# Attention scores: full-array matmuls with stacked high and low parts, local and context keys in one matmul, two heads' half-array matmuls in a row

## The chip, the core and the metric

The kernel runs on one core of a Trainium2 chip. A core has five engines that each take their instructions in order: TensorE (PE in the profile, its weight loads PEld), VectorE (DVE), ScalarE (ACT), GpSimd (POOL) and SyncE (SP), which here issues most DMAs. The metric is the device time of one execution in microseconds; lower is better.

## What is computed

Two layers over 512 latent tokens (a grid of 8 rows and 64 columns) and 256 context tokens, width 1024. Each layer has a mixer and a gated MLP. The first layer's mixer is a state-space scan beside neighbourhood attention (8 heads of 64 channels), the second's is differential attention (8 heads, each with two sub-heads of 64 channels). All data is float32. The parts that the change touches, cut short:

```
def neighbourhood_attention(q, k, v, k_ctx, v_ctx, rpb):
    # each latent query sees an 8 x 16 window of the grid and all context keys
    s_loc = einsum('bqhd,bjqkhd->bhqjk', q_r, k_r) * dh ** -0.5 + bias
    s_ctx = einsum('bqhd,bkhd->bhqk', q_r, k_ctx) * dh ** -0.5
    p = softmax(concatenate([s_loc, s_ctx], -1))
    return einsum(p_loc, v_r) + einsum(p_ctx, v_ctx)

def dense_attention(q, k, v):            # context queries, context keys
    s = einsum('bqhd,bkhd->bhqk', q, k) * dh ** -0.5
    return einsum('bhqk,bkhd->bqhd', softmax(s), v)

def diff_attend(q, k, v, lam):           # 512 queries, 768 keys
    s = einsum('bqhd,bkhd->bhqk', q, k) * DIFF_SUB_DIM ** -0.5
    p = softmax(s).reshape(b, DIFF_HEADS, 2, lq, nk)
    a = p[:, :, 0] - lam * p[:, :, 1]
    return einsum('bhqk,bkhd->bqhd', a, v)
```

## The kernel before

**Precision by parts.** The matmuls of projections and scores read a rounded 32-bit type (float32r). To keep float32 accuracy an operand is split into a high part (the rounded value) and a low part (the rest), and products are summed as high x high + low x high + high x low. A score has only 64 channels to contract, half of the array's 128 rows. So `split_qk` (neighbourhood) and `d_qk` (differential) stack parts on the rows: for the head on half e, the tile `Q[e]` holds q's high part on that half and its low part on the other, and `Kh[e]` holds k's high part on both halves. One matmul over all 128 rows then gives high x high + low x high. The third product, high q x low k, is a second matmul over the 64 rows of that half alone, with the low parts of both heads in one tile, `Kl`. It is a half-array matmul: 64*128 in the rows of the profile, where the others have 128*128.

**Neighbourhood attention.** The latent tokens are kept column block by column block, so a block of 128 queries needs two consecutive chunks of keys. `na_pair` works on two heads: four blocks of latent queries (local keys, then 256 context keys) and two of context queries (context keys alone), six units in all, each done by `na_unit`. For each head a unit takes a bank of PSUM for `S`, computes the scores segment by segment (L717, L718), adds the bias (L722, `bt`, NEG outside the window), does the softmax (L725 to L728), transposes it in place (L733) and copies it to `Pt` (L742). Both heads' products with V then go into the first head's bank (L750), and `out` copies them to `att` (L768) and stores them. The local segment has 192 keys in the first and last block and 256 in the others. Before, the first head's instructions all stand ahead of the second's.

**Stages.** In the loop over four groups of state-space heads, `ssd_group` of one group, `na_pair` of the group before (pairs 0 to 2) and, as filler, the projections of the next are written in turns. `na_pair` has two PSUM banks there, three for pair 2. The last pair runs after the loop with two banks and three more in turn, beside the output projection. Then come the first gated MLP, the differential attention and the second MLP.

**Differential attention.** `d_qk(h)` projects and rotates q and k of a head one head ahead, and splits them on ScalarE, VectorE and GpSimd. `d_head(h)` takes the 512 queries in four blocks: for each sub-head a tile `dSp` of 768 scores in two matmuls of 512 and 256 keys with `Kh` (L1188) and two with `Kl` (L1191), then the softmax, the difference, transposes and the product with V.

**What sets the order.** A planner orders each engine's instructions at build time by priority (mostly the order in which the code is written), dependences, free buffers and its own estimate of times. `nc.any` lets it choose ScalarE or VectorE for a copy.

Of the kernel before, what the change touches and what calls it, by code (L numbers as in the profile page):

```python
# [21 lines left out]
NX = 512  # L22
# [29 lines left out]
# Engines (ScalarE, VectorE, GpSimd) of a layer norm's affine map, high parts and low parts.  # L52
# [7 lines left out]
class Ring:  # L60
    """Tiles of several pools in turn, as if of one pool."""
# [10 lines left out]
def emit(tc, T):  # L72
# [16 lines left out]
    pmm = Ring(*MM)  # L89

# [343 lines left out]
    # SSD: time steps and decays  # L434
# [234 lines left out]
    # neighbourhood attention  # L669
# [39 lines left out]

    def na_unit(Q, Kh, Kl, V, qo, segs, chunks, bias, out, pool, tp_, nb):  # L710
        n = sum(m for _, m in segs)
        Ss = []
        for e in range(2):
            S = pool[0].tile([128, 512], F32, name="S", tag=pool[1])
            o = 0
            for k0, m in segs:
                nc.tensor.matmul(S[:, o:o + m], Q[e][:, qo:qo + 128], Kh[e][:, k0:k0 + m], start=True, stop=False)  # L717
                nc.tensor.matmul(S[:, o:o + m], Q[e][HALF[e], qo:qo + 128], Kl[HALF[e], k0:k0 + m], start=False, stop=True)  # L718
                o += m
            if bias is not None:  # L720
                m = segs[0][1]
# [3 lines left out]
            nc.vector.tensor_reduce(nm[:, 0:1], S[:, 0:n], axis=AX, op=OP.max, negate=True)  # L725
            nc.scalar.activation(P[:, 0:n], S[:, 0:n], AF.Exp, bias=nm[:, 0:1], accum_out=nm[:, 1:2])
# [3 lines left out]
            o = 0  # L730
            for i, c in enumerate(chunks):
                m = toks[c][1]
                nc.tensor.transpose(PT[0:m, i], P[:, o:o + m], ident)  # L733
                o += m
# [18 lines left out]
    def na_pair(p, q, k, v, pools, tp_=None, nb=2):  # L753
# [17 lines left out]
        for b in range(4):  # L771
            chunks, k0, nl = NA_BLOCKS[b]
            bt = tp_.tile([128, 2, 256], F32, name="bt", bufs=nb // 2)
            nc.sync.dma_start(bt, T["na_bias"][p, b])
            na_unit(*QK, V, 128 * b, [(k0, nl), (512, 256)], chunks + (5, 6), bt,
# [3 lines left out]
        for t in range(2):  # L779
            na_unit(*QK, V, 512 + 128 * t, [(512, 256)], (5, 6), None,  # L780
# [360 lines left out]

    def rot(px, scale, r):
# [10 lines left out]
    def d_qk(h):  # L1153
# [11 lines left out]
        Kh = [dp.tile([128, NT], F32R, name=f"Kh{e}", bufs=2) for e in range(2)]  # L1165
        Kl = dp.tile([128, NT], F32R, name="Kl", bufs=2)
# [6 lines left out]
        Q = [dp.tile([128, NX], F32R, name=f"Q{e}", bufs=2) for e in range(2)]  # L1173
# [3 lines left out]
        return Q, Kh, Kl  # L1177

    def d_head(h, Q, Kh, Kl, V, filler=()):
        filler = iter(filler)  # L1180
        ob = dp.tile([128, 4, 128], F32, name="ob", bufs=3)
        for tt in range(4):
            ts = slice(128 * tt, 128 * tt + 128)
            Ss = [pS.tile([128, 1024], F32, name="dSp", tag="S") for e in range(2)]
            cols = ((0, 512), (512, 256))
# [159 lines left out]
def _na_bias(rpb):  # L1345
    out = np.full((8, 4, 128, 256), NEG, np.float32)
    qi = np.arange(128)
    for b in range(4):
        _, k0, nl = NA_BLOCKS[b]
        qt = 128 * b + qi  # L1350
        kt = k0 + np.arange(nl)
# [6 lines left out]
        g = rpb[:, dr, dc]  # L1358
        out[:, b, :, 256 - nl:] = np.where(ok[None], g, np.float32(NEG))
# [66 lines left out]
```

## Time and profile before

| | us |
|---|---|
| median of 3 runs | 2067.78 |
| fastest and slowest run | 2060.84, 2069.96 |
| the profiled execution: span from the first to the last instruction | 2062.4 |
| in it: PE busy | 1986.9 |
| DVE busy | 1388.2 |
| ACT busy | 897.9 |
| POOL busy | 754.1 |

Of the profiled execution the page gives the span alone. Matmuls are pipelined: the duration of one in the profile is its latency, and several run at once, so what one costs a full queue is the time from its start to the next one's start. In the timeline a row with x2 stands for two matmuls in a row; its first number is the start of the first, and the next row's first number is the start of the one behind. "Idle before" in brackets names what ended an engine's wait.

### The profile page before, as it was taken

How to read it: one execution, taken by the hardware profiler on the slowest of the kernel's cores; microseconds unless marked ns; L12 is line 12 of the kernel's file. 1: busy time of each engine (PE TensorE's matmuls, PEld its weight loads, DVE VectorE, ACT ScalarE, POOL GpSimd, SP SyncE). 2: the span in 40 equal slices, each digit the busy share in tenths (PEclk: the TensorE clock that was granted, in tenths of full speed). 3: DMA queues.
4: the chain of work that ended last, by engine and by line, in shares of the span. 5: the costliest groups of instructions: out<-in, count | busy, mean ns of one | idle time of the engine just before them, and what ended most of it. 6: DMA issues, size and time to landing. Idle time of an engine off the chain costs nothing.

```text
span 2062.4 us, 31227 instructions
## 1 busy us (share of the span) xinstructions
PE 1986.9 (96%) x11992; PEld 1663.9 (81%) x11992; DVE 1388.2 (67%) x2199; ACT 897.9 (44%) x1757; POOL 754.1 (37%) x631
## 2 busy tenths in 40 slices
PE   7999999999998889999999999999999999999998
PEld 5888878888676787788888888888888778888886
DVE  3766565664757987887676677766556876655567
ACT  3545555574532532223222233655655644333332
POOL 2135124243415935444444417521115264222223
PEclk9999999999999999999999999999999999999999
DMA  9335332232523144333343341322112214323231
GB/s 308 120 107 177 98 122 76 72 121 78 202 72 105 54 135 131 116 100 113 102 143 103 102 144 52 121 62 74 57 51 86 87 42 135 113 82 102 82 113 62
DMA packets 109301, 217.60 MB, mean 106 GB/s; under 512 B 27096, under 2 KB 45888, under 8 KB 109152
## 3 DMA queue, kind: packets, MB, share of 16 engines
q1 hardware_dynamic: 98480, 189.44, 28.6%
q0 software_dynamic: 6016, 20.03, 2.9%
q10 hardware_dynamic: 4656, 6.13, 1.0%
q8 instruction: 95, 1.56, 0.3%
q14 instruction: 54, 0.44, 0.1%
HBM read 202.81 MB, written 8.55 MB: 102 GB/s over the span
## 4 chain that ended last, share of the span: by engine, by line
PE 81%; DVE 11%; DMA 3%; issue 2%; POOL 1%; ACT 1%; SPq 0%; DVEq 0%; ACTq 0%; POOLq 0%
PE fpx L292 20%; PE pdn L1015 13%; PE px L292 7%; PE fpc L292 5%; PE pv L308 4%; PE pc L292 3%; PE pz L308 3%; PE po L833 3%; PE pk L292 2%; PE pq L292 2%; PE S L750 2%; PE avp L1212 2%; DVE acc L185 2%; DMA araw<-in_ada_w 2%; PE dSp L1191 2%
## 5 line engine op out<-in xcount | busy, mean ns | idle before, releaser
L139 ACT ACTIVATE whi<-raw 128x1024 fp32r<-128x1024 f32 (+1 forms) x205 | 215.5, 1057 | 447.7 <-PE fpc L292 163.1
L140 DVE TENSOR_TENSOR wlo<-raw,whi 128x1024 fp32r<-128x1024 f32 (+1 forms) x192 | 256.0, 1339 | 164.0 <-ACT whi L139 161.6
L1015 PE MATMUL pdn<-whi,fact 128*128 128x512 f32 x880 | 280.0, 399 | 5.6 <-DVE ev L314 5.6
L316 POOL TENSOR_TENSOR y<-y,ev 128x512 f32<-128x512 f32 x144 | 211.7, 1485 | 197.3 <-DVE ev L314 153.1
L292 PE MATMUL fpx<-ux,whi 128*128 128x512 f32 (+1 forms) x832 | 232.3, 364 | 6.1 <-DVE cv L974 3.3
L292 PE MATMUL fpx<-u,whi 128*128 128x512 f32 (+1 forms) x832 | 227.4, 359 | 2.4 <-DVE cv L974 1.5
L1015 PEld LDWEIGHTS pdn<-whi,fact 128*128 128x128 f32 x880 | 162.5, 188 | 45.1 <-DVE ev L314 7.0
L292 PEld LDWEIGHTS fpx<-ux,whi 128*128 128x128 f32 x832 | 149.4, 192 | 30.7 <-issue 5.3
L1015 PE MATMUL pdn<-wlo,fact 128*128 128x512 f32 x440 | 172.9, 395 | 0.0
L999 POOL TENSOR_TENSOR fact<-cv,fact 128x768 fp32r<-128x768 f32 (+1 forms) x44 | 73.3, 1666 | 272.4 <-ACT fact L998 272.4
L292 PEld LDWEIGHTS fpx<-u,whi 128*128 128x128 f32 x832 | 149.2, 191 | 26.2 <-ACT cv L970 1.6
L292 PE MATMUL fpx<-ux,wlo 128*128 128x512 f32 (+1 forms) x416 | 151.3, 364 | 2.9 <-DVE wlo L140 2.9
L292 PE MATMUL fpx<-u,wlo 128*128 128x512 f32 (+1 forms) x416 | 149.1, 359 | 1.1 <-DVE wlo L140 1.1
L292 PE MATMUL px<-ux,whi 128*128 128x512 f32 x448 | 149.4, 406 | 0.3 <-ACT whi L139 0.2
L185 DVE SCALAR_TENSOR_TENSOR acc<-araw,condp,acc 128x512 f32<-128x512 f32 x140 | 133.1, 976 | 22.8 <-DMA araw<-in_ada_w 22.2
L974 DVE SCALAR_TENSOR_TENSOR cv<-fpx,fcw,cv 128x511 f32<-128x511 f32 x176 | 130.4, 744 | 22.3 <-ACT cv L970 21.0
L138 POOL TENSOR_TENSOR raw<-raw,G 128x1024 f32<-128x1024 f32 x30 | 76.8, 2565 | 173.7 <-DMA raw<-in_w_down 71.8
L292 PE MATMUL fpc<-uc,whi 128*128 128x256 f32 x704 | 130.3, 283 | 2.0 <-DVE uc L362 1.3
L292 PEld LDWEIGHTS fpc<-uc,whi 128*128 128x128 f32 x704 | 112.4, 190 | 6.7 <-DVE uc L362 1.5
L367 POOL TENSOR_TENSOR y<-y,gb 128x256 f32<-128x256 f32 x112 | 103.5, 959 | 28.1 <-PE lntp L346 28.1
L314 DVE SCALAR_TENSOR_TENSOR ev<-pdn,G 128x512 f32<-128x512 f32 x120 | 81.7, 683 | 41.4 <-PE pdn L1015 34.8
L292 PE MATMUL fpc<-uc,wlo 128*128 128x256 f32 x352 | 99.5, 283 | 0.0
(328 smaller groups left out, 4639.2 us busy)
## 6 DMA issues: line engine op xcount, KB each, us to landing
araw<-in_ada_w SPq DMA_DIRECT2D x96, 512.0 KB
raw<-in_w_up SPq DMA_DIRECT2D x88, 512.0 KB
raw<-in_w_down SPq DMA_DIRECT2D x44, 512.0 KB
E<-scr POOLq DMA_DIRECT2D x24, 512.0 KB, 4.7
raw<-in_w_dqk SPq DMA_DIRECT2D x16, 512.0 KB
raw<-in_w_qkv SPq DMA_DIRECT2D x12, 512.0 KB
raw<-in_w_out SPq DMA_DIRECT2D x12, 512.0 KB
raw<-in_w_bc SPq DMA_DIRECT2D x8, 512.0 KB
```

The costliest lines, as they stand in the source:

```text
L138: nc.gpsimd.tensor_tensor(raw, raw, gate, op=OP.mult)
L139: nc.scalar.activation(hi[:, :n], raw[:, :n], AF.Copy)
L140: (eng or nc.vector).tensor_tensor(lo[:, :n], raw[:, :n], hi[:, :n].bitcast(F32), op=OP.subtract)
L185: nc.vector.scalar_tensor_tensor(acc[:, s], raw[:, i], cs, acc[:, s], op0=OP.mult, op1=OP.add)
L292: nc.tensor.matmul(ps, w[wi][:, kc], rhs(kc, ui), start=(i == 0), stop=(i == n - 1))
L308: nc.tensor.matmul(ps, u_dst(u, kc, ui, tt), w[kc // 4][wi][:, kc % 4], start=(i == 0), stop=(i == n - 1))
L314: nc.vector.scalar_tensor_tensor(t, ps, r, Gh, op0=OP.mult, op1=OP.mult)
L316: eng.tensor_tensor(yh, yh, t, op=OP.add)
L367: nc.gpsimd.tensor_tensor(y[:, c:c + 256], y[:, c:c + 256], t[:, c:c + 256], op=op)
L974: nc.vector.scalar_tensor_tensor(dst[:, lo:hi_], src[:, lo + d:hi_ + d], f[:, tap:tap + 1], dst[:, lo:hi_], op0=OP.mult, op1=OP.add)
L999: nc.gpsimd.tensor_tensor(at_[:, 1], val, at_[:, 0].bitcast(F32), op=OP.subtract)
L1015: nc.tensor.matmul(ps, acts[2 * gs[0] + kt][:, ui, 128 * tt:128 * tt + 128], ws[kt][wi][:, 0, o:o + 512], start=(m == 0), stop=(m == 3 * n ...
```

## The change

In `na_unit` both heads' banks are taken at the start. Each head's first matmul (L717) takes local and context keys together, 512 columns, through a two-part access pattern (`keys`), so the local part always has 256 keys; the fourth block's softmax leaves its first 64 columns out (`NA_COLS`), the first block's takes all 512, with NEG in the bias where the window ends. The two half-array matmuls (L718), one for each head, come after both heads' first ones; `behind` is a dependence that only the planner sees, without a semaphore. `na_bias` is filled for 256 keys in every block.

In `d_qk` the roles change: K's tile now has the high part on the head's own half and the low part on the other; `Qh` has q's high part on both halves, and `Ql` q's low part on the head's half and zeros on the other. `d_head` then uses full-array matmuls only, `Qh` and `Ql` against the same `K`. The zero halves are set once, in four tiles that heads use in turn (`Qlow`). Comments are dropped, which moves the line numbers: L717 and L718 become L731 and L733, L1188 and L1191 become L1210.

```
-NA_BLOCKS = [((0, 1), 0, 192), ((1, 2), 64, 256), ((2, 3), 192, 256), ((3, 4), 320, 192)]
+NA_BLOCKS = [((0, 1), 0), ((1, 2), 64), ((2, 3), 192), ((3, 4), 256)]
+NA_COLS = [(0, 512), (0, 512), (0, 512), (64, 448)]
...
+    def behind(later, earlier):
+        tc.add_manual_dep(later.ins, earlier.ins.name,
+                          mybir.DependencyInfo(mybir.DependencyClass.NoSync, mybir.DependencyReason.DATA), reason="issue order")
...
+    def keys(t, rows, k0):
+        v = t[rows, k0:k0 + 256]
+        return bass.AP(tensor=v.tensor, offset=v.offset, ap=[v.ap[0], [NX - k0, 2], [1, 256]])
+
-    def na_unit(Q, Kh, Kl, V, qo, segs, chunks, bias, out, pool, tp_, nb):
-        n = sum(m for _, m in segs)
+    def na_unit(Q, Kh, Kl, V, qo, k0, chunks, bias, out, pool, tp_, nb):
+        ctx = k0 is None
+        c0, n = (512 - 256, 256) if ctx else NA_COLS[qo // 128]
+        kr = (lambda t, rows: t[rows, NX:NT]) if ctx else (lambda t, rows: keys(t, rows, k0))
+        full = slice(0, 128)
+        S2 = [pool[0].tile([128, 512], F32, name="S", tag=pool[1]) for _ in range(2)]
+        so = [S[:, 256:512] if ctx else S for S in S2]
+        for e in range(2):
+            hi = nc.tensor.matmul(so[e], Q[e][:, qo:qo + 128], kr(Kh[e], full), start=True, stop=False)
+        for e in range(2):
+            lo = nc.tensor.matmul(so[e], Q[e][HALF[e], qo:qo + 128], kr(Kl, HALF[e]), start=False, stop=True)
+            behind(lo, hi)
         Ss = []
         for e in range(2):
-            S = pool[0].tile([128, 512], F32, name="S", tag=pool[1])
-            o = 0
-            for k0, m in segs:
-                nc.tensor.matmul(S[:, o:o + m], Q[e][:, qo:qo + 128], Kh[e][:, k0:k0 + m], start=True, stop=False)
-                nc.tensor.matmul(S[:, o:o + m], Q[e][HALF[e], qo:qo + 128], Kl[HALF[e], k0:k0 + m], start=False, stop=True)
-                o += m
+            S = S2[e]
+            sv = S[:, c0:c0 + n]
             if bias is not None:
-                nc.vector.tensor_tensor(S[:, 0:m], S[:, 0:m], bias[:, e, 256 - m:256], op=OP.add)
+                nc.vector.tensor_tensor(S[:, c0:256], S[:, c0:256], bias[:, e, c0:256], op=OP.add)
...
+    Qlow = [[dp.tile([128, NX], F32R, name=f"Ql{i}{e}") for e in range(2)] for i in range(2)]
+    for i in range(2):
+        for e in range(2):
+            nc.gpsimd.memset(Qlow[i][e][HALF[1 - e]].bitcast(F32), 0.0)
...
-            nc.scalar.copy(Kh[e][HALF[e]], rk[HALF[e]])
-            nc.any.tensor_copy(Kh[e][HALF[1 - e]], Kh[e][HALF[e]].bitcast(F32))
-            nc.gpsimd.tensor_tensor(Kl[HALF[e]], rk[HALF[e]], Kh[e][HALF[e]].bitcast(F32), op=OP.subtract)
+            nc.scalar.copy(K[e][HALF[e]], rk[HALF[e]])
+            nc.gpsimd.tensor_tensor(K[e][HALF[1 - e]], rk[HALF[e]], K[e][HALF[e]].bitcast(F32), op=OP.subtract)
...
-            nc.scalar.copy(Q[e][HALF[e]], rq[HALF[e]])
-            nc.vector.tensor_tensor(Q[e][HALF[1 - e]], rq[HALF[e]], Q[e][HALF[e]].bitcast(F32), op=OP.subtract)
+            nc.scalar.copy(Qh[e][HALF[e]], rq[HALF[e]])
+            nc.any.tensor_copy(Qh[e][HALF[1 - e]], Qh[e][HALF[e]].bitcast(F32))
+            nc.vector.tensor_tensor(Ql[e][HALF[e]], rq[HALF[e]], Qh[e][HALF[e]].bitcast(F32), op=OP.subtract)
...
             for e in range(2):
-                for o, m in cols:
-                    nc.tensor.matmul(Ss[e][:, o:o + m], Q[e][:, ts], Kh[e][:, o:o + m], start=True, stop=False)
-            for o, m in cols:
-                for e in range(2):
-                    nc.tensor.matmul(Ss[e][:, o:o + m], Q[e][HALF[e], ts], Kl[HALF[e], o:o + m], start=False, stop=True)
+                for o, m in ((0, 512), (512, 256)):
+                    for i in range(2):
+                        nc.tensor.matmul(Ss[e][:, o:o + m], Q[i][e][:, ts], K[e][:, o:o + m], start=(i == 0), stop=(i == 1))
```

How the planner's order moves, first on the PE at the first unit of the first pair. nQ_2293 and nQ_2294 are the two heads' Q. Before:

```order
L621 MATMUL Sps<-xw,Bt 128x256
L717 MATMUL S<-nKh_2290,nQ_2293 128x192
L718 MATMUL S<-nKl,nQ_2293 128x192
L717 MATMUL S<-nKh_2290,nQ_2293 128x256
L718 MATMUL S<-nKl,nQ_2293 128x256
L717 MATMUL S<-nKh_2291,nQ_2294 128x192
L718 MATMUL S<-nKl,nQ_2294 128x192
L717 MATMUL S<-nKh_2291,nQ_2294 128x256
L718 MATMUL S<-nKl,nQ_2294 128x256
L620 MATMUL Sps<-xw,Bt 128x256
```

and now, on the same engine at the same place:

```order
L629 MATMUL Sps<-xw,Bt 128x256
L731 MATMUL S<-nKh_2290,nQ_2293 128x512
L731 MATMUL S<-nKh_2291,nQ_2294 128x512
L733 MATMUL S<-nKl,nQ_2293 128x512
L733 MATMUL S<-nKl,nQ_2294 128x512
L628 MATMUL Sps<-xw,Bt 128x256
```

Eight matmuls became four, and the change between full and half array is made once where it was made four times. In most later units of the loop the second head's high matmul stands 10 to 17 rows behind the first head's, as the second head's did before, and the two low ones follow it at once.

On the PE at the first block of head 0 of the differential attention, Q_12794 and Q_12795 being the two sub-heads' Q. Before:

```order
L1188 MATMUL dSp<-Kh_12774,Q_12794 128x512
L1188 MATMUL dSp<-Kh_12774,Q_12794 128x256
L1191 MATMUL dSp<-Kl,Q_12794 128x512
L1191 MATMUL dSp<-Kl,Q_12794 128x256
L292 MATMUL pq<-ux,wlo 128x256
```

and now, on the same engine, K_12718 being the first sub-head's K:

```order
L1210 MATMUL dSp<-K_12718,Qh_12735 128x512
L1210 MATMUL dSp<-K_12718,Ql_12562 128x512
L1210 MATMUL dSp<-K_12718,Qh_12735 128x256
L1210 MATMUL dSp<-K_12718,Ql_12562 128x256
L316 MATMUL pv<-wlo,ux 128x256
```

The count is the same, four; the half-array ones are gone, and the two that share a range of columns stand together.

On VectorE, at the preparation of head 0's Q (rq is the rotated q, wlo a weight's low part, dnm the first softmax's maximum). Before:

```order
L1151 TENSOR_TENSOR rq<-rq,qsw 128x512
L140 TENSOR_TENSOR wlo<-raw,whi 128x1024
L1176 TENSOR_TENSOR Q_12794<-rq,Q_12794 64x512
L1176 TENSOR_TENSOR Q_12795<-rq,Q_12795 64x512
L1196 TENSOR_REDUCE dnm<-dSp 128x1
```

and now, on the same engine:

```order
L1173 TENSOR_TENSOR rq<-rq,qsw 128x512
L148 TENSOR_TENSOR wlo<-raw,whi 128x1024
L1198 TENSOR_TENSOR Ql_12562<-rq,Qh_12735 64x512
L1197 CAST Qh_12735<-Qh_12735 64x512
L1198 TENSOR_TENSOR Ql_12563<-rq,Qh_12736 64x512
L1197 CAST Qh_12736<-Qh_12736 64x512
L1215 TENSOR_REDUCE dnm<-dSp 128x1
```

Two copies have come in between the subtractions and the first softmax.

## Rows read from the trace of the kernel before

**Rows 1.** The page: the span, and each engine's busy time and share.

```profile
span 2062.4 us, 31227 instructions
...
PE 1986.9 (96%) x11992; PEld 1663.9 (81%) x11992; DVE 1388.2 (67%) x2199; ACT 897.9 (44%) x1757; POOL 754.1 (37%) x631
```

**Rows 2.** Stretches: length, busy PE, PEld, DVE, ACT, POOL, then clock, DMA share, GB/s.

```profile
210.00:540.00 330.00, 325.67 (x2064) 270.87 (x2062) 205.30 (x453) 192.42 (x463) 112.90 (x144) 0.99 0.31 100
540.00:630.00 90.00, 89.18 (x437) 67.38 (x437) 48.26 (x97) 36.04 (x91) 21.36 (x17) 0.96 0.37 122
690.00:1345.00 655.00, 631.07 (x3667) 542.21 (x3668) 500.47 (x683) 219.00 (x354) 297.52 (x211) 0.98 0.36 113
1345.00:1640.00 295.00, 293.54 (x1815) 244.28 (x1814) 193.11 (x270) 173.65 (x380) 74.39 (x41) 1.00 0.20 62
```

**Rows 3.** Timeline, PE, differential attention: start, length (us), line, out<-in, array, shape, count.

```profile
1381.31 0.40 PE L292 MATMUL dpc<-uc,whi 128*128 128x256 f32 x2
1381.55 0.51 PE L1188 MATMUL dSp<-Kh,Q 128*128 128x512 f32 x2
1381.99 0.61 PE L1191 MATMUL dSp<-Kl,Q 64*128 64x512 f32 x2
1382.53 0.39 PE L292 MATMUL dpc<-uc,wlo 128*128 128x256 f32 x1
1382.76 0.40 PE L292 MATMUL dpc<-uc,whi 128*128 128x256 f32 x2
```

**Rows 4.** Timeline of the same stretch, the PE's weight loads.

```profile
1381.43 0.31 PEld L1188 LDWEIGHTS dSp<-Kh,Q 128*128 128x128 f32 x2
1381.99 0.29 PEld L1191 LDWEIGHTS dSp<-Kl,Q 64*128 64x128 f32 x2 [0.25 <-issue]
```

**Rows 5.** Timeline, PE, a projection in the differential attention.

```profile
1386.31 0.62 PE L292 MATMUL pq<-ux,whi 128*128 128x512 f32 x2
1386.76 0.39 PE L292 MATMUL pq<-ux,wlo 128*128 128x512 f32 x1
```

**Rows 6.** Timeline, PE, the second unit of the first pair, and the third's start.

```profile
234.61 0.39 PE L717 MATMUL S<-nKh,nQ 128*128 128x256 f32 x1
...
235.87 0.38 PE L292 MATMUL pc<-uc,wlo 128*128 128x256 f32 x1
236.09 0.40 PE L292 MATMUL pc<-uc,whi 128*128 128x256 f32 x2
...
238.31 0.36 PE L717 MATMUL S<-nKh,nQ 128*128 128x256 f32 x1
...
253.00 0.39 PE L717 MATMUL S<-nKh,nQ 128*128 128x256 f32 x1
```

**Rows 7.** Timeline, PE, one head of a unit of context queries.

```profile
310.94 0.28 PE L717 MATMUL S<-nKh,nQ 128*128 128x256 f32 x1
311.15 0.38 PE L718 MATMUL S<-nKl,nQ 64*128 64x256 f32 x1
311.46 0.39 PE L292 MATMUL pc<-uc,whi 128*128 128x256 f32 x1
311.69 0.28 PE L292 MATMUL pc<-uc,wlo 128*128 128x256 f32 x1
```

**Rows 8.** Timeline, PE, where both sub-heads' half-array matmuls stand in a row.

```profile
1588.49 0.62 PE L1191 MATMUL dSp<-Kl,Q 64*128 64x512 f32 x4
1589.04 0.73 PE L1261 MATMUL dpo<-whi,dact 128*128 128x512 f32 x2
```

**Rows 9.** Line L1191: count, least/median/greatest ns, first and last start, forms.

```profile
L1191 PE MATMUL dSp<-Kl,Q x128: 271/438/501, 1350.3 to 1635.0; 64*128 64x512 f32 x64, 64*128 64x256 f32 x64
```

**Rows 10.** Lines on ACT and DVE, as rows 9; then POOL's timeline.

```profile
L768 ACT COPY att<-S x24: 238/266/278, 234.8 to 625.5; 128x128 f32<-128x128 f32 x24
L1175 ACT CAST Q<-rq x16: 616/618/622, 1347.8 to 1597.9; 64x512 fp32r<-64x512 f32 x16
L725 DVE TENSOR_REDUCE nm<-S x48: 412/616/692, 218.3 to 613.1; 128x1 f32<-128x448 f32 x16, 128x1 f32<-128x512 f32 x16, 128x1 f32<-128x256 f32 x16
1333.54 1.30 POOL L1150 TENSOR_TENSOR qsw<-qsw,rope 128x512 f32<-128x512 f32 x1 [22.57 <-DVE wlo L140]
```

More of the change, by code (lines that the diff above doesn't have):

```diff
@@ L708, in split_qk @@
         return Q, Kh, Kl
[L710 to L711 removed]
+    def keys(t, rows, k0):
[13 more added lines that the diff above has]
+            behind(lo, hi)
         Ss = []
         for e in range(2):
[L714 to L719 removed]
+            S = S2[e]
+            sv = S[:, c0:c0 + n]
             if bias is not None:
[L721 to L722 removed]
+                nc.vector.tensor_tensor(S[:, c0:256], S[:, c0:256], bias[:, e, c0:256], op=OP.add)
             P = tp_.tile([128, 512], F32, name="P", bufs=nb)
             nm = tp_.tile([128, 2], F32, name="nm", bufs=2 * nb)
[L725 to L726 removed]
+            nc.vector.tensor_reduce(nm[:, 0:1], sv, axis=AX, op=OP.max, negate=True)
+            nc.scalar.activation(P[:, 0:n], sv, AF.Exp, bias=nm[:, 0:1], accum_out=nm[:, 1:2])
             nc.vector.reciprocal(nm[:, 1:2], nm[:, 1:2])
@@ L729, in na_unit @@
             PT = S.rearrange("p (c q) -> p c q", q=128)
-            o = 0
             for i, c in enumerate(chunks):
-                m = toks[c][1]
+                t0, m = toks[c]
+                o = (t0 - (256 if t0 >= NX else k0)) - c0
                 nc.tensor.transpose(PT[0:m, i], P[:, o:o + m], ident)
-                o += m
             Pt = tp_.tile([128, 4, 128], F32, name="Pt", bufs=nb)
@@ L771, in na_pair @@
         for b in range(4):
-            chunks, k0, nl = NA_BLOCKS[b]
+            chunks, k0 = NA_BLOCKS[b]
             bt = tp_.tile([128, 2, 256], F32, name="bt", bufs=nb // 2)
             nc.sync.dma_start(bt, T["na_bias"][p, b])
-            na_unit(*QK, V, 128 * b, [(k0, nl), (512, 256)], chunks + (5, 6), bt,
+            na_unit(*QK, V, 128 * b, k0, chunks + (5, 6), bt,
                     lambda av: out(128 * b, av),
@@ L779, in na_pair @@
         for t in range(2):
-            na_unit(*QK, V, 512 + 128 * t, [(512, 256)], (5, 6), None,
+            na_unit(*QK, V, 512 + 128 * t, None, (5, 6), None,
                     lambda av: out(512 + 128 * t, av), pools[t % len(pools)], tp_, nb)
@@ L1164, in d_qk, with d_head @@
         ct_x(pq, w, u, 2 if h < 2 else 1)
-        Kh = [dp.tile([128, NT], F32R, name=f"Kh{e}", bufs=2) for e in range(2)]
-        Kl = dp.tile([128, NT], F32R, name="Kl", bufs=2)
+        K = [dp.tile([128, NT], F32R, name=f"K{e}", bufs=2) for e in range(2)]
         for e in range(2):
-            nc.scalar.copy(Kh[e][HALF[e]], rk[HALF[e]])
-            nc.any.tensor_copy(Kh[e][HALF[1 - e]], Kh[e][HALF[e]].bitcast(F32))
-            nc.gpsimd.tensor_tensor(Kl[HALF[e]], rk[HALF[e]], Kh[e][HALF[e]].bitcast(F32), op=OP.subtract)
+            nc.scalar.copy(K[e][HALF[e]], rk[HALF[e]])
+            nc.gpsimd.tensor_tensor(K[e][HALF[1 - e]], rk[HALF[e]], K[e][HALF[e]].bitcast(F32), op=OP.subtract)
         rq = dp.tile([128, NX], F32, name="rq", tag="rq", bufs=1)
         rot(pq, 0.125, rq)
-        Q = [dp.tile([128, NX], F32R, name=f"Q{e}", bufs=2) for e in range(2)]
+        Qh = [dp.tile([128, NX], F32R, name=f"Qh{e}", bufs=2) for e in range(2)]
+        Ql = Qlow[h % 2]
         for e in range(2):
-            nc.scalar.copy(Q[e][HALF[e]], rq[HALF[e]])
-            nc.vector.tensor_tensor(Q[e][HALF[1 - e]], rq[HALF[e]], Q[e][HALF[e]].bitcast(F32), op=OP.subtract)
-        return Q, Kh, Kl
-    def d_head(h, Q, Kh, Kl, V, filler=()):
+            nc.scalar.copy(Qh[e][HALF[e]], rq[HALF[e]])
+            nc.any.tensor_copy(Qh[e][HALF[1 - e]], Qh[e][HALF[e]].bitcast(F32))
+            nc.vector.tensor_tensor(Ql[e][HALF[e]], rq[HALF[e]], Qh[e][HALF[e]].bitcast(F32), op=OP.subtract)
+        return (Qh, Ql), K
+    def d_head(h, Q, K, V, filler=()):
         filler = iter(filler)
@@ L1348, in _na_bias @@
     for b in range(4):
-        _, k0, nl = NA_BLOCKS[b]
+        chunks, k0 = NA_BLOCKS[b]
         qt = 128 * b + qi
-        kt = k0 + np.arange(nl)
+        kt = k0 + np.arange(256)
         qr, qc = (qt // 8) % 8, (qt // 64) * 8 + qt % 8
@@ L1357, in _na_bias @@
         dc = np.where(ok, kcol[None, :] - qc[:, None] + 15, 0)
-        g = rpb[:, dr, dc]
-        out[:, b, :, 256 - nl:] = np.where(ok[None], g, np.float32(NEG))
+        out[:, b] = np.where(ok[None], rpb[:, dr, dc], np.float32(NEG))
     return out
```

1 line of the change is left out of this document (removed).

## The prediction

> **What bounds the kernel now.** I read the page first: TensorE is busy for 1986.9 of 2062.4 us, the next engine, VectorE, for 67% [rows 1]. An average can hide a stage with another limit, so the second view is the busy time by stretch. The changed matmuls stand in three stretches: the hybrid layer's loop (210 to 540 us), the last pair of neighbourhood heads (540 to 630) and the differential attention (1345 to 1640). In all three the PE is idle for 4.3, 0.8 and 1.5 us, and VectorE and ScalarE are busy for no more than 66% [rows 2]. The granted clock there is 0.96 to 1.00 of the 2.4 GHz level, so a slower clock has little to give back. In these stretches time is what the PE needs to issue, and a matmul that goes is time that goes, unless a wait takes its place.
>
> "Busy" counts pipelined latencies, so I price a matmul from start to start in the timeline. In a stream of full-array matmuls a 512-column one takes 0.227 us (two in 0.45, [rows 5]) and a 256-column one 0.12 (two in 0.24, the first of [rows 3]). A matmul on half of the rows breaks the stream. Kh's 256 columns are followed after 0.21 instead of 0.12 (310.94 to 311.15, [rows 7]), the half-array one by the next after 0.31, and that next one, full again, takes 0.23 instead of 0.12. The weight loads show why: in the stream a load starts ahead of its matmul (1381.43 for 1381.55), at the change it starts with it (1381.99) [rows 4]. So going to half costs 0.09, coming back the rest.
>
> **The change, part by part.**
>
> *Differential attention.* Before: for a head half and a block of 128 queries, two full matmuls (512 and 256 columns) and two half ones. From 1381.55 to the next foreign matmul at 1382.53 it is 0.98 us, and that next one takes 0.11 too long: 1.09. There are 128 half matmuls [rows 9], two a set, so 64 sets: 69.8 us. After: four full matmuls, 2 x 0.227 + 2 x 0.12 = 0.69, 64 times: 44.4. Gain 25.4 us. The stationary operand whose other half is zero costs what any full one costs.
>
> That price needs each of the four weight loads to be hidden; row 1381.43 shows two of them hidden in the same place [rows 4]. The Trainium skill ("TensorE: Matmul & The Clock Gate", Part 3, on what overlaps) says that a weight load overlaps a running matmul only when the row group differs. The trace does not agree for full-array streams. By that rule the four matmuls would pay their loads in the open, and the sum for this stage would be a loss of some 3 us; it is a rival below.
>
> *Neighbourhood units with local keys.* There are 4 pairs x 4 blocks = 16 units, two heads each. Before, a head's set is full, half, full, half: 234.61 to 235.87 = 1.26 us, and the next matmul takes 0.22 instead of 0.12 [rows 6]: 1.36. 32 sets: 43.5 us (16 have a local part of 192 columns, a little less; I take 43). After: one 512-column full matmul for each head, then both heads' half ones. The first full one 0.227; the second 0.227 + 0.09 for the change. For the two half ones the trace has one place where halves of both heads stand in a row: four of them, 512 and 256 columns for each head, take 0.55 us from 1588.49 to 1589.04 [rows 8], where one head's two alone take 0.54 (1381.99 to 1382.53). So halves on different rows run at once; less 0.12 for the pair of 256, a pair of 512 takes 0.43. With 0.10 for the matmul behind: 0.23 + 0.32 + 0.43 + 0.10 = 1.08, 16 times: 17.3 us. Gain 25.7.
>
> *Units of context queries.* 4 pairs x 2 = 8. Before, a head's full and half matmul: 0.52 us and 0.11 behind [rows 7], 16 sets: 10.1. After: 0.12 + 0.21 + 0.31 + 0.11 = 0.75, 8 times: 6.0. Gain 4.1.
>
> Together 25.4 + 25.7 + 4.1 = 55 us of PE time. About three quarters of the neighbourhood part, 22 us, is in the loop, a quarter, 7.5, in the last pair.
>
> *What the change adds.* (1) Both heads' S banks must be free before the low matmuls, since each stands behind both high ones. The first head's bank of a unit comes free only with the copy of the previous unit's output, 0.27 us [rows 10]; what is queued behind the waiting matmul on the PE is everything, filler too. In the loop, with two banks (three for the third pair) and 18 units, I charge each unit that copy and 0.08 for the handover: 18 x 0.35 = 6.3 us. From below it is zero (in most units the order has 10 to 17 rows of other matmuls between the two high ones, as before between the heads), from above 3.7 us a unit (rival 3). I take 6.3, because other matmuls mostly stand in between, but the next unit's start is already tied to that copy: 234.61 is within 0.5 us of it. The last pair has five banks; no charge. (2) Differential attention copies Qh's second half where it copied Kh's: 64x512 instead of 64x768, two a head, so ScalarE and VectorE get less. But Q ends the first head's preparation, and in the order VectorE now has the two copies between the subtractions: 2 x 0.62, ScalarE's price for a tile of that size [rows 10], = 1.2 us, once; later heads are prepared a head ahead. (3) GpSimd's low part of K is now wanted by the first matmul, not the second; its time was the same size before, and K is done ahead of Q. (4) Four memsets on GpSimd for the zero halves: ahead of the first rotation GpSimd idles for 22.57 us [rows 10], which hides them; with that cover gone they would stand in front of the rotation. (5) In 8 softmaxes a row is 64 columns longer: a reduction goes from 0.41 to 0.69 us for 256 columns more [rows 10], so 0.07 on VectorE, and about that in three more steps on VectorE and ScalarE; both have about a third free. (6) The planner sets a new order for the whole middle of the kernel; on SP, bias loads move ahead of a weight load by a place or two. The first gated MLP, whose code is unchanged, has 24 us of PE idle time [rows 2]; I take 0, and 6 us to either side for the range.
>
> Net: 55 - 6.3 - 1.2 = 47.5 us. The profiled execution's span is 2062.4, and 2062.4 - 47.5 = 2014.9. The median of the runs is 2067.8, 5.4 above that span; I forecast in its terms: **2020 us**.
>
> **The rivals.**
>
> 1. *The loop is held by its chain.* If softmax, copies and states set the pace there, the PE's 22 us become idle time. For it: a unit's first matmul follows the last unit's only after 18.4 us (234.61 and 253.00, [rows 6]), so six units and their preparation fill most of a third of the 330 us. Against: the PE has 4.3 us of idle time in 330, while a chain that held it would show as waits. It would leave 47.5 - (22 - 6.3) = 31.8 of gain: 2036 us.
>
> 2. *Weight loads of full-array matmuls come into the open* where two different weights alternate on one set of columns. Each of the 256 matmuls of differential attention would take 0.11 more, the exposed load of [rows 3]: 28 us, so 2048. Against it: high and low weights alternate in [rows 5], at 0.227 each. The Trainium skill's page on TensorE, cited above, would have it so.
>
> 3. *Slower: the PE stands in front of the low matmuls.* Now the second head starts 3.7 us after the first (234.61 and 238.31, [rows 6]). If the PE really waited that long for the second bank in each of the 24 units, it would lose 89 us: 2067.8 + 89 - 55 = 2102. It decides from 55/24 = 2.3 us a unit. For it: PE is in order. Against: the order puts other work into that gap.
>
> 4. *The change does not do what it says:* the halves of the two heads do not overlap. In the order they stand in a row in 23 of 24 units, and four ran at once in [rows 8]; but if not, each unit pays one more half matmul and its load, 0.34 for 512 and 0.23 for 256 columns: 16 x 0.34 + 8 x 0.23 = 7.3, so 2027.
>
> **How the numbers follow.** Forecast 0.72, rival 1 0.14, rival 2 0.04, rival 3 0.05, rival 4 0.05. The predicted time is the forecast's, 2020. Its own bounds: no charge for the banks gives 2014, with 6 us of luck in the order 2008; bad order and twice the charge give 2032. The range for 8 in 10 goes on to rival 1 with its 6 us of order: 2006 to 2042. What a measurement can tell from no change is about 0.5%, 10 us. Faster by more: all but rival 3 and some of rival 2 with bad order, 0.91; within it 0.04; slower 0.05.
>
> **What would show it right or wrong.** In the timeline after, a set of four full matmuls of dSp should take 0.69 us to the next, and all should be 128 rows; the four S matmuls of a unit about 1.0, the two low ones starting within 0.01 us of each other. The stretch of differential attention should be shorter by about 24 us, the loop by about 16, the last pair by about 7, and the first and second MLP by nothing. PE idle in the loop should stay under 12 us. If it grows by 20 or more, with S's high matmul waiting for the copy of the output, rivals 1 or 3 hold; if weight loads of dSp start with their matmul, rival 2; if the low matmuls start 0.3 us apart, rival 4. The forecast is wrong if the MLP stretches change by more than 6 us, since I priced the new order there at nothing.

## The result and the profile after

| | before | after |
|---|---|---|
| median (4 runs each, us) | 2068.87 | 2037.17 |
| lowest, highest | 2060.84, 2070.79 | 2033.74, 2041.21 |
| ratio, 95% interval | | 0.9851, 0.9831 to 0.9872 |
| span of the profiled execution | 2062.4 | 2033.0 |

The kernel became 31.7 us faster by the medians and 29.4 by the profiled spans, where 47.5 was forecast. The time lies inside the range, but a third of the gain is missing. The page of the kernel after, which answers to [rows 1]:

```profile
span 2033.0 us, 31103 instructions
...
PE 1937.5 (95%) x11928; PEld 1649.1 (81%) x11928; DVE 1383.6 (68%) x2202; ACT 893.9 (44%) x1756; POOL 752.2 (37%) x635
```

The PE's busy time fell by 49.4 us. Some of it ran at half clock: the mean granted clock was 0.988 before and 0.984 after. By the clock records of the two traces the PE was busy at the lower level for 39.8 us before and 50.3 after in all; half of that is lost, 19.9 and 25.1 us. At full clock the PE's work therefore fell by about 55 us, and 55 was forecast. So the prices of the matmuls were right in sum. Idle time took 20.0 us of the gain (75.5 to 95.5) and the clock about 5.

Where that happened is read by stages, cut at the same events in both kernels (not at fixed times as [rows 2]): first score S, last matmul of the latent projections, first matmul of the first MLP, first and last dSp, first matmul of the second MLP. Stretches of before: length, busy PE, granted clock, DMA share, GB/s.

```profile
0.00:215.50 215.50, 195.54 (x1849) 0.99 0.54 175
215.50:502.20 286.70, 286.70 (x1834) 1.00 0.30 97
502.20:693.60 191.40, 176.54 (x883) 0.97 0.32 106
693.60:1349.90 656.30, 635.30 (x3704) 0.98 0.36 112
1349.90:1635.00 285.10, 283.63 (x1743) 1.00 0.20 62
1635.00:1680.60 45.60, 39.64 (x207) 0.96 0.18 64
1680.60:2062.40 381.80, 369.54 (x1787) 0.99 0.30 99
```

The same stages of the kernel after:

```profile
0.00:218.00 218.00, 195.70 (x1848) 0.99 0.53 173
218.00:484.70 266.70, 265.20 (x1779) 1.00 0.32 103
484.70:674.10 189.40, 169.76 (x874) 0.93 0.33 111
674.10:1327.10 653.00, 633.16 (x3709) 0.99 0.35 112
1327.10:1598.20 271.10, 261.56 (x1732) 0.99 0.21 63
1598.20:1649.80 51.60, 42.06 (x215) 0.93 0.17 66
1649.80:2033.00 383.20, 370.10 (x1787) 0.99 0.29 98
```

| stage | forecast | measured |
|---|---|---|
| up to the first score | 0 | +2.5 |
| loop, last pair and output | -15.7 - 7.5 = -23.2 | -22.0 |
| first MLP, first projections | 0 | -3.3 |
| differential attention, first to last score | -24.2 | -14.0 |
| from the last score to the second MLP | 0 | +6.0 |
| second MLP | 0 | +1.4 |

The second and third stretch are compared by their sum, since the cut between them does not fall at the same work: before, 50 of the 80 high matmuls of S stand ahead of it, after, 28 of 48. So the neighbourhood part gave what was forecast, within what executions differ by: from the first score to the first MLP before takes 478.1 us, and d_only (below), with the same matmuls in the same order up to there, 482.5; after takes 456.1, and five more executions with its order there (after_again, na_only, d_rows, a_ob, a_keep, all below) 456.6 to 458.2. The differential attention with its end gave 8.0 of 24.2. In the third, fifth and sixth stretch the PE's idle time (length less busy) grew from 14.9 to 19.6, from 1.5 to 9.5 and from 6.0 to 9.5 us, and the clock fell in all three.

The single prices hold. Timeline of the PE, a set of four full matmuls of dSp, to be held against [rows 3]; under it the first weight load inside the set:

```profile
1383.98 0.39 PE L1210 MATMUL dSp<-K,Qh 128*128 128x512 f32 x1
1384.21 0.39 PE L1210 MATMUL dSp<-K,Ql 128*128 128x512 f32 x1
1384.44 0.28 PE L1210 MATMUL dSp<-K,Qh 128*128 128x256 f32 x1
1384.56 0.28 PE L1210 MATMUL dSp<-K,Ql 128*128 128x256 f32 x1
1384.68 0.40 PE L300 MATMUL pk<-ux,wlo 128*128 128x512 f32 x1
```

```profile
1383.98 0.19 PEld L1210 LDWEIGHTS dSp<-K,Ql 128*128 128x128 f32 x1
```

From 1383.98 to 1384.68 is 0.70 us (0.69 forecast). The load for Ql starts at 1383.98, one matmul ahead of the matmul that needs it at 1384.21, so it is hidden. The rule of the Trainium skill ("TensorE: Matmul & The Clock Gate", Part 3, what overlaps and what doesn't), that a weight load overlaps a running matmul only on another row group, does not hold for these rows: both use all rows.

A neighbourhood unit's second head and both low matmuls, to be held against [rows 6]:

```profile
258.01 0.40 PE L731 MATMUL S<-nKh,nQ 128*128 128x512 f32 x1
258.34 0.50 PE L733 MATMUL S<-nKl,nQ 64*128 64x512 f32 x2
258.77 0.50 PE L300 MATMUL px<-ux,whi 128*128 128x512 f32 x1
259.11 0.40 PE L300 MATMUL px<-ux,wlo 128*128 128x512 f32 x1
```

The pair of halves takes 0.43 us, as derived from [rows 8], so the halves run at once. High 0.33, halves 0.43, the matmul behind 0.34 instead of 0.23; with the first head's own high matmul that is close to the 1.08 forecast.

### The profile page after: what moved, and what is told of

It reads as the page before. It is cut to its first block, busy times and chain, and to the rows that moved or that the text cites. A ratio compares the mean times of both kernels' runs of the same rounds, so it can differ in the third digit from the quotient of the medians.

```text
span 2033.0 us, 31103 instructions
## 1 busy us (share of the span) xinstructions
PE 1937.5 (95%) x11928; PEld 1649.1 (81%) x11928; DVE 1383.6 (68%) x2202; ACT 893.9 (44%) x1756; POOL 752.2 (37%) x635
## 5 line engine op out<-in xcount | busy, mean ns | idle before, releaser
L987 ACT ACTIVATE cv<-fpx,fcw 128x512 f32<-128x512 f32 x88 | 67.6, 770 | 79.7 <-PE fpx L300 77.4
```

Of the source, the lines that this page charges most:

```text
L987: nc.scalar.activation(dst, src, AF.Identity, bias=f[:, 3:4], scale=f[:, 1:2])
```

## Experiments

**Each half of the change alone.** `na_only` has the new `na_unit` with the old differential attention, `d_only` the other way round; the edits are the two halves of the diff shown ahead:

```
na_only:  na_unit, keys, behind, NA_BLOCKS as after;  d_qk, d_head as before (no Qlow)
d_only:   d_qk, d_head, Qlow as after;  na_unit, NA_BLOCKS as before
```

> The neighbourhood part of the change alone; the differential attention is that of before. In the trace after, this part gave 17.4 us by the end of the loop, 2 in the last pair and 3.3 in the first gated MLP. Theory (saved PE time is kept where the PE finds other work to pull in, and is lost at the ends of stages, where chains over other engines and DMAs set the time): those three again, about 22 us less than before, ratio 0.989, time 2046. Rival (the lost part is chance of the planner's new order, not of a place): any sum from 15 to 30 is possible, with the last pair and the MLP not repeating their 2 and 3.3 us. Price of the prediction for this part: 23.5 less.

> The differential part alone; the neighbourhood part is that of before. Theory: the stretch from the first to the last scores becomes 14 us shorter, the stretch from there to the second MLP 6 longer, so 8 to 10 us less than before, ratio 0.9955, time 2060. Rival (what was lost in this stage came from the order that the other part had shifted): the whole PE saving of 24 us shows, ratio 0.988, time 2044.

Measured: na_only 2044.96 us, ratio 0.9884 (0.9863 to 0.9905); d_only 2050.60, ratio 0.9913 (0.9895 to 0.9932); before beside them 2070.54. By the ratios that is 24.0 and 18.0 us (25.6 and 19.9 by the medians), where the prediction's terms for them are 23.5 and 24.2. The sum of the two is 42.0; both together, at 0.9851, give 30.8 of that median. So the neighbourhood half loses nothing by itself, the differential half some 6 us, and another 11 go missing when they meet (each of the three ratios is good to about 4 us). The time of na_only fits its theory (22 us) and the price alike; the 3.3 us of the first MLP did not come again (657.8 for 656.3). My theory for d_only fell: it gained about twice the 8 to 10 us. Its stretches from the first to the last score and on to the second MLP:

```profile
1356.20:1616.50 260.30, 257.98 (x1731) 1.00 0.21 65
1616.50:1667.50 51.00, 42.32 (x216) 0.93 0.19 66
```

311.3 us together, against 330.7 before and 322.7 after, with the same instructions of this stage as after, up to a few records. What differs is their order. The planner gave the PE in this stage of the kernel after an order that departs in about 100 places from that of d_only, though the code of the stage is the same.

**The order of the four matmuls.** In `na_split` each head's low matmul stands behind its own high one; `d_rows` keeps the operands of before in the differential attention and forces the halves of both sub-heads into a row:

```
 na_split, na_unit:
         for e in range(2):
             hi = nc.tensor.matmul(so[e], Q[e][:, qo:qo + 128], kr(Kh[e], full), ...)
-        for e in range(2):
             lo = nc.tensor.matmul(so[e], Q[e][HALF[e], qo:qo + 128], kr(Kl, HALF[e]), ...)
             behind(lo, hi)
 d_rows, d_head, against before (d_qk as before):
             for o, m in cols:
                 for e in range(2):
-                    nc.tensor.matmul(Ss[e][:, o:o + m], Q[e][HALF[e], ts], Kl[HALF[e], o:o + m], ...)
+                    lo = nc.tensor.matmul(Ss[e][:, o:o + m], Q[e][HALF[e], ts], Kl[HALF[e], o:o + m], ...)
+                    behind(lo, hi)          # hi: the last full matmul of both sub-heads
```

> The kernel after, with local and context keys still in one matmul, but each head's half-array matmul right behind its own full one, so that the halves don't run at once and the second head waits for no bank of the first. By PE prices a unit with local keys costs 0.6 us more, one of context queries 0.5: 16 x 0.6 + 8 x 0.5 = 13.6 us. Theory: the loop's three quarters of it are lost in full, the last pair's quarter in part: 10 to 14 us slower than the kernel after, 2047 to 2051, ratio 0.990 to 0.992 against before. Rival 1 (merging the keys is the gain, the row of halves gives nothing): 0 to 3 us slower than after. Rival 2 (waiting for both banks costs what the prediction charged, 6 us): only about 8 us slower.

> The kernel after with the operands of before in the differential attention (Q stacked, K's high part on both halves, its low part in a tile of its own), but the half-array matmuls of both sub-heads forced into a row behind all four full ones. By PE prices a block of two sub-heads costs 1.43 us where four full ones each cost 1.39: 32 x 0.04 = 1.3 us more. Theory that PE time is all that counts here: 0 to 3 us slower than after. Rival: the first sub-head's softmax now waits for the second's tile, and that chain sets the time: 8 to 25 us slower than after. Second rival (the copies of Q's high part, which fall away here, were what the stage lost): 3 to 6 us faster than after.

Measured: na_split 2042.50 us, ratio 0.9873 (0.9853 to 0.9894); d_rows 2036.14, 0.9842 (0.9821 to 0.9863). The two stretches of the differential attention of na_split:

```profile
1344.70:1604.60 259.90, 257.75 (x1731) 1.00 0.21 66
1604.60:1655.50 50.90, 41.04 (x215) 0.97 0.20 68
```

Its first MLP starts 15.7 us later than that of after (689.8 for 674.1), where 13.6 were computed: the row of halves is worth its price, and waiting for both banks costs little. But by the end only 4 to 5 us of that are left (the theory had 10 to 14), since the differential attention with its end takes 310.8 us. In this kernel the planner's order there is that of d_only, matmul for matmul. The operands stacked as before with the halves in a row (d_rows) cost the same time as four full matmuls, and the rival of 8 to 25 us is out. In the two stretches the PE is busy for 306.5 us there and for 303.6 after, where 1.3 more were priced; its stage has an order of its own, so the two can't be told apart more closely than by the few us that an order makes.

**The planner's order by itself.** `p3split` is the kernel after with na_split's edit in the last pair alone:

```
+        split = cur[0] == 3            # set by na_pair to its pair
         for e in range(2):
             hi = nc.tensor.matmul(so[e], Q[e][:, qo:qo + 128], kr(Kh[e], full), ...)
+            if split:
+                lo = nc.tensor.matmul(so[e], Q[e][HALF[e], qo:qo + 128], kr(Kl, HALF[e]), ...)
-        for e in range(2):
+        for e in range(0 if split else 2):
             lo = nc.tensor.matmul(so[e], Q[e][HALF[e], qo:qo + 128], kr(Kl, HALF[e]), ...)
```

> The kernel after, but in the last neighbourhood pair each head's half-array matmul stands right behind its own full one. By PE prices that costs 4 x 0.6 + 2 x 0.5 = 3.4 us. It also makes the planner give the PE, from the first gated MLP on, another order than in the kernel after: in the differential attention the very one of d_only and na_split, where the stretch from the first scores to the first projection of the second MLP took 311.3 and 310.8 us; in the kernel after it took 322.7. Theory (the missing gain of the prediction is that order, with its waits and the low clock behind them): that stretch takes 311, the whole is 6 to 10 us faster than the kernel after, 2028 to 2032, ratio 0.980 to 0.982. Rival 1 (chains at the end of the stage give back whatever the PE saves; d_only was long on time because it came later): the stretch stays at 320 or more, and the whole is 2 to 4 us slower than after, 2040. Rival 2 (the last pair gains nothing from halves in a row, since it is held by its chain): 3 us better than the theory.

Measured: 2033.26 us, ratio 0.9825 (0.9806 to 0.9845). The two stretches, which took 322.7 us after:

```profile
1336.20:1598.80 262.60, 258.38 (x1732) 1.00 0.22 66
1598.80:1648.90 50.10, 40.84 (x215) 0.97 0.19 68
```

312.7 us, close to the theory's 311, and rival 1 is out: the same code in the other order takes 10 us less. That p3split comes to this stage 9 us later doesn't explain it: a repeated run of after (after_again, below) comes to it at 1333.7, within 3 us of p3split, and takes 321.5. The whole gained less than expected (5 us by the ratios, whose intervals overlap): the last pair and the output together took 193.3 us instead of 189.4, near the 3.4 us of the PE's price, which speaks against rival 2, and the way from the first MLP to the first score 658.2 instead of 653.0. In that last stage executions of one kernel scatter by some 4 us (after_again: 657.0).

What the order does, in the trace: three long waits, 7.4 us in all, stand in the differential attention of the kernel after that d_only does not have; its idle time there is 2.3 us, that of after 9.5. Timeline of the PE after, rows with a wait, and the stretch around the longest:

```profile
1417.27 0.47 PE L1210 MATMUL dSp<-K,Qh 128*128 128x512 f32 x1 [1.09 <-ACT Qh L1197]
...
1420.88 0.47 PE L1210 MATMUL dSp<-K,Qh 128*128 128x512 f32 x1 [1.80 <-ACT Qh L1197]
...
1557.76 1.22 PE L1280 MATMUL dpo<-whi,dact 128*128 128x512 f32 x2 [4.55 <-ACT qraw L1166]
```

```profile
1556.00:1564.00 8.00, 6.24 (x16) 0.57 0.14 34
```

The clock was at its lower level for most of these 8 us (mean granted clock 0.57). The longest wait has a chain of causes. The output projection dpo (L1280) needs the bank of pq, which ScalarE copies out (L1166). GpSimd and ScalarE ahead of it, after:

```profile
1545.51 2.40 POOL L146 TENSOR_TENSOR raw<-raw,G 128x1024 f32<-128x1024 f32 x1 [2.08 <-DMA raw<-in_w_do]
1549.97 2.40 POOL L146 TENSOR_TENSOR raw<-raw,G 128x1024 f32<-128x1024 f32 x1 [2.06 <-DMA raw<-in_w_do]
1552.32 1.04 POOL L1258 TENSOR_TENSOR ob<-ob,rso 128x512 f32<-128x512 f32 x1
1553.32 1.26 POOL L1172 TENSOR_TENSOR qsw<-qsw,rope 128x512 f32<-128x512 f32 x1
```

```profile
1555.40 1.68 ACT L1189 CAST K<-rk 64x768 fp32r<-64x768 f32 x2 [8.64 <-DVE rk L1173]
1557.11 0.60 ACT L1166 ACTIVATE qraw<-pq 128x512 f32<-128x512 f32 x1
```

ScalarE's queue is in order: the copy of pq stands behind K's high parts, these wait 8.64 us for the rotated k, the rotation for GpSimd's multiply (L1172), and that stands behind two gate multiplies of w_do, each of which waits 2 us for a load. In d_only the same ScalarE row waits 2.00 us:

```profile
1573.91 1.69 ACT L1172 CAST K<-rk 64x768 fp32r<-64x768 f32 x2 [2.00 <-DVE rk L1156]
```

and its output projection waits for nothing. This chain is read from the trace; no experiment moved the gate multiplies alone. So it is shown that the order costs some 10 us, and only argued by which waits.

**The end of the stage.** In every kernel with the new differential attention the stretch from the last score to the second MLP is 2 to 7 us longer than the 45.6 us of before and na_only; less than 1 us of that is eight more matmuls that fall behind the cut. In the kernel after the PE waits there twice for the stored outputs of two heads (ob), their scaling and transposes (1615.31, idle 4.19 us, and 1623.14, 1.56). `a_ob` issues the loads of ob on another queue, `p3s_ob` does so in p3split, and `a_keep` and `p3s_keep` leave head 5's output in its buffer:

```
 a_ob, p3s_ob, d_prep:
-                nc.sync.dma_start(ob, scrO[h + i])
+                nc.scalar.dma_start(ob, scrO[h + i])
 a_keep, p3s_keep:
-        if h < 6:
+        if h < 5:
             nc.scalar.dma_start(scrO[h], ob)
-            acts = d_prep(4)
+            acts = d_prep(4, [None, ob5])     # ob5: head 5's tile
```

> The kernel after, with one edit: the loads of stored attention outputs (ob from scrO, six of them) are issued on ScalarE's DMA queue instead of SyncE's, where the last of them stands behind loads of weights whose buffers are freed late. The PE's order up to the differential attention is that of after. Theory (this queue makes the wait of 4.19 us ahead of the transposes near 1615 us and the low clock behind it): the wait falls below 1.5 us, and the whole is 4 to 7 us faster than after, 2030 to 2033. Rival (the wait goes to the next chain, such as the weights of the output projection or the row sums): 0 to 2 us faster. Second rival (the issue on ScalarE holds up the copies behind it): 0 to 5 us slower.

> Both edits, that of p3split and the loads on ScalarE's queue; the planner then gives the differential attention a third order. Theory, if both hold and this order brings no new wait: 10 to 16 us faster than after, 2021 to 2027. Rival (any new order of this stage brings waits of its own, 5 to 10 us of them): 2028 to 2035.

Measured: a_ob 2033.51 us, ratio 0.9836 (0.9813 to 0.9859); p3s_ob 2036.74, 0.9854 (0.9835 to 0.9873). The queue was not the cause. VectorE in a_ob:

```profile
1614.53 0.69 DVE L1258 TENSOR_TENSOR ob<-ob,rso 128x512 f32<-128x512 f32 x1 [3.35 <-DMA ob<-scrO]
```

The load was issued no earlier, at 1608.08 on ScalarE's queue (after: 1607.99 on SyncE's), and landed 6.4 us later, so the PE's wait only fell to 3.18. The gain of a_ob is within what two executions differ by. p3s_ob has a third order of the stage (317.5 us for the two stretches, 312.7 in p3split), with waits of its own (2.02 us ahead of a transpose at 1545.51, which p3split does not have), as its rival said; the time lies beyond even the rival's 2035.

> In the kernel with the loads on ScalarE's queue the last load of ob was still issued at 1608.1 us, only once the buffer that it fills had been given back by the output projection of the heads before, and landed 6.4 us later; a wait of 3.18 us stayed. Here, in the kernel after, head 5's outputs stay in the buffer in which they were made, and are neither stored nor loaded again; 24 rows of the PE's order in the differential attention move, all at its end. Theory (this load is what the end of the stage waits for, once the PE comes earlier): the wait of 4.19 us ahead of the transposes and the half clock behind it go, the stretch from the last scores to the second MLP falls from 51.6 to about 46, the whole is 4 to 7 us faster than the kernel after, 2030 to 2033. Rival (the next chain there, the row sums through VectorE and ScalarE, takes its place): 0 to 2 us.

> The same edit on the kernel whose last neighbourhood pair has its halves apart (p3split), where the order of the differential attention is that of d_only. Theory: the two gains add, so 4 to 7 us faster than p3split, 2026 to 2029, ratio 0.979 to 0.981, the fastest so far; the stretch from the first scores to the second MLP, 312.7 in p3split, falls to 306 to 308. Rival: 0 to 2 us, stretch 311 or more.

Measured: a_keep 2031.42 us, ratio 0.9837 (0.9814 to 0.9859); p3s_keep 2029.19, 0.9826 (0.9806 to 0.9846). The last stretch fell from 51.6 to 47.8 and from 50.1 to 47.5 us: about 3, between theory and rival. The whole is 2.9 us faster than after by the ratios for a_keep; p3s_keep has the ratio of p3split, so there the gain shows in the stretch and not in the time. The wait for the load is gone and the next chain, the row sums, is in its place; VectorE in a repeated run of p3s_keep (best_again), then the PE:

```profile
1614.40 0.17 DVE L1254 TENSOR_SCALAR rso<-dss 128x8 f32<-128x8 f32 x1 [4.97 <-ACT dsq L1243]
```

```profile
1617.20 1.94 PE L1271 MATMUL otp<-c_consts,ob 128*128 128x128 f32 x8 [3.41 <-DVE ob L1267]
```

**After and the best, side by side.** Both unchanged:

```
after_again = the kernel after;  best_again = p3s_keep
```

> The kernel after once more, unchanged, to compare it with the next one beside the same runs of before. Theory that the profiled executions compared so far are typical: median 2033 to 2038, and again a wait of 4 to 5 us ahead of the output projection near 1555 us, one of 3 to 4 ahead of the transposes near 1613 us, and the stretch from the first scores of the differential attention to the second MLP at 322 us within 2. Rival (the 322.7 was one bad execution, and not the order): 312 to 316.

> The kernel p3s_keep once more, unchanged: halves apart in the last pair, head 5's outputs kept. Theory: 6 to 8 us faster than the kernel after beside it, the stretch from the first scores to the second MLP at 309.7 within 2. Rival (the difference between them was chance of the executions): within 3 us of it.

Measured: after_again 2036.59 us, ratio 0.9851 (0.9829 to 0.9872); best_again 2027.94, 0.9812 (0.9795 to 0.9830). All four runs of the one (2034.25 to 2039.64) lie above all of the other (2027.22 to 2028.43): 8.6 us. The stretches of after_again are 270.8 and 50.7 us, 321.5 together, with the same wait of 4.56 us ahead of the output projection, so the 322.7 us were no accident of one execution. Those of best_again:

```profile
1335.30:1595.60 260.30, 258.00 (x1731) 1.00 0.21 65
1595.60:1644.30 48.70, 41.13 (x215) 0.93 0.19 65
```

309.0 us. This kernel is faster than before and than after, though it puts back a part of the change that costs 3.4 us of PE time: the planner's order that comes with it is worth some 10, and the kept output some 3 in the last stretch.

## Why the prediction was right and where it was wrong

- *What bounds the kernel, and the prices.* Right. The PE lost about 55 us of work for 55 forecast; sets of dSp take 0.70 us, pairs of halves 0.43. Rival 2 (loads in the open) and rival 4 (no overlap) are out by the rows above.
- *Charge (1), both banks, 6.3 us.* Its cause was wrong and its size right by luck. Up to the last latent projection the PE's idle time is 1.5 us after and 0.0 before: the other matmuls between the two high ones cover the copy, also at the units' starts, and rival 3, the slower one, never came near its 2.3 us a unit. But up to the first MLP idle time grew by 6.3 us all the same (14.9 to 21.1), from waits that the prediction did not have.
- *The last pair, "five banks; no charge".* This step failed, though the sum of the neighbourhood part came out. Five banks were no protection, since it was not the banks. Behind the loop the PE waits for VectorE, once for the states' factors and twice for the softmax; the two longest waits stand at the end, for ScalarE's copy of att ahead of the output projection and for VectorE's y ahead of the last transposes (timeline of the PE after, rows with the long waits, and two stretches behind the first three):

```profile
504.75 0.49 PE L650 MATMUL gp<-xc 128*128 128x128 f32 x2 [2.82 <-DVE t L660]
...
508.17 1.09 PE L751 MATMUL S<-c_consts,P 128*128 128x128 f32 x4 [1.70 <-DVE P L746]
...
534.81 0.66 PE L751 MATMUL S<-c_consts,P 128*128 128x128 f32 x2 [3.48 <-DVE nm L745]
...
628.33 1.22 PE L943 MATMUL po<-whi,att 128*128 128x512 f32 x2 [3.84 <-ACT att L911]
...
672.46 0.87 PE L354 MATMUL lntp<-c_consts,y 128*128 128x128 f32 x3 [5.63 <-DVE y L350]
```

```profile
505.00:512.00 7.00, 5.19 (x20) 0.52 0.02 6
533.00:543.00 10.00, 7.16 (x25) 0.51 0.23 76
```

  p3split has the first three too (2.82, 2.78 and 3.48 us), with its halves apart in this pair, so the row of halves in this pair doesn't make them; na_split, whose PE comes 12 us later, has none of them. That fits an earlier PE that meets VectorE's chain, rival 1's mechanism at another place than I put it, but no run took that chain away. The two at the end are in after_again as well (4.33 and 5.58 us) and not in before, na_split or p3split (1.2 us at most at these places), so they come with the order that the row of halves brings; what makes them was not tested.
- *Copies of Qh for later heads, priced at nothing* since heads are prepared ahead. In the kernel after ScalarE makes them late at head 3, 1.09 and 1.80 us of waiting. In d_only the PE does not wait for the same copies, so it is the order, and not the copies.
- *Point (6), the order, 0 with 6 us to either side, weighed in the first MLP only.* This was the largest miss. The first MLP's stage became 3.3 us shorter, which is within its scatter, but in the differential attention with its end the order cost 10 us against the one that p3split got. With d_only's order that stage alone gives 24.8 us (285.1 to 260.3), and 24.2 were forecast, so its price was right and its order was not. The stage also has a limit at its end that I gave no price: 4 to 6 us there, of which some 3 are the reloaded output, and the row sums stand behind it.
- *The range.* The forecast's own range ended at 2032; the time fell inside the wider one through rival 1's 2036. That 2037 is so close to it is luck: rival 1 has the loop held by its chain, and up to the last latent projection the PE waited for 1.5 us.
- *Waits were priced at their length.* Many long ones also cost clock (below): about 5 us of the 18 that are missing.

## What to carry to other kernels

Where a planner sets the order, a change is priced in two parts: the work that it takes away, and the order that it makes elsewhere, which can cost 10 us in a stage whose code is the same. To tell the two apart, run each half of the change alone and compare the orders stage by stage; gains that don't add point to the order. When an engine that is busy 96% of the time gets less to do, look ahead for the places with nothing to pull in (the end of a loop, of a stage), and charge the next chain there, and the clock that a long wait can cost.

## What the runs showed of the hardware

A long wait of the PE can cost more than its length. At or behind most of the PE's longer waits the granted clock was at the lower of its two levels (1.2 of 2.4 GHz), for a time that differs between executions of the same instructions. d_only has the very program of before up to the differential attention, and both wait about as long at one place (PE, before and then d_only):

```profile
530.22 1.82 PE L650 MATMUL op<-PV,xc 128*128 128x256 f32 x4 [3.23 <-DVE xD L662]
```

```profile
531.49 2.07 PE L650 MATMUL op<-PV,xc 128*128 128x256 f32 x4 [3.12 <-DVE xD L662]
```

The stretches there at the lower level, first in before, then in d_only:

```profile
530.50:534.00 3.50, 3.50 (x15) 0.51 0.11 37
```

```profile
530.00:554.00 24.00, 22.42 (x79) 0.50 0.29 87
```

At this wait d_only is 1.3 us behind before, at the start of the first MLP 5.8 (699.4 for 693.6): 4.5 us, with the same matmuls in the same order and no more idle time in that stage (14.9 and 14.4 us), so from the clock. The mean clock of that whole stage, 0.97 of 191.4 us in before and 0.94 of 195.9 in d_only, gives 6. The Trainium skill ("TensorE: Matmul & The Clock Gate", Part 1, HAM oscillation) counts half of the time at the low level as lost, which is of that size. The scatter of before goes with it for the most part: of 36 executions the ten shortest (2059.7 to 2063.0 us) had mean clocks of 0.987 to 0.991, the ten longest (2068.8 to 2071.1) 0.981 to 0.986; one of 2067.3 us, with 0.989, does not fit. The execution profiled for the prediction, with 0.988, was one of the shorter ones.
